# A hybrid recurrent decoder step: the recurrence's rates as their own branch, its scans four a step, the last mLSTM pair one granule later

## The chip, the cores and the metric

The kernel runs on one core of a Trainium2 chip. The metric is the device time of one execution in microseconds (us). The core has a matrix engine (TensorE, PE in the profile; its weight loads are listed as PEld), a vector engine (VectorE, DVE), a scalar engine for activation functions (ScalarE, ACT), a general engine (GpSimd, POOL) and an engine that issues transfers (SyncE, SP). Each takes its own instructions in the order in which the program hands them over, and waits on semaphores that other engines and transfers raise. The 16 DMA engines serve the transfers of all queues.

## The reference

One inference step of a layer of a decoder, for 256 tokens of a prompt and 8 x 4 tokens of samples, 288 columns in all. Three branches share one projection `w_in`, and each is weighed by its own sigmoid gate before `w_out`; an MLP follows.

```python
proj = xn @ P['w_in']                       # D_MODEL = 2048
u, lru_conv_new = causal_conv(lru_x, lru_conv, P['lru_conv_w'], P['lru_conv_b'])
y_lru, lru_h_new = rglru(u, lru_h, ...)
...
h, C_new, n_new, m_new = mlstm_chunked(mq, mk, mv, gates[..., :MLSTM_HEADS], gates[..., MLSTM_HEADS:], ml_C, ml_n, ml_m)
y_ml = jax.nn.sigmoid(m_o) * rmsnorm(h.astype(dt), P['ml_g_norm']).reshape(B, T, MLSTM_WIDTH)
merged = (gate[:, :, 0] * (y_lru @ P['w_br_lru']) + gate[:, :, 1] * (y_gla @ P['w_br_gla'])
          + gate[:, :, 2] * (y_ml @ P['w_br_ml']))
```

The recurrence (RG-LRU) is, per channel,

```python
r = jax.nn.sigmoid((blockdiag(x, w_a) + b_a).astype(f32))
i = jax.nn.sigmoid((blockdiag(x, w_x) + b_x).astype(f32))
log_a = LRU_C * r * jax.nn.log_sigmoid(lam.astype(f32))
a = jnp.exp(log_a)
u = jnp.sqrt(-jnp.expm1(2.0 * log_a)) * (i * x.astype(f32))
# h_t = a_t * h_{t-1} + u_t
```

The factor `log_sigmoid(lam)` depends on weights alone; it is what the kernel calls the rates. The mLSTM branch keeps a matrix memory C of 256 x 256 for each of 4 heads and 8 samples, which is read, used and written back.

## The kernel before

**Layout.** Features lie on the 128 partitions, the 288 columns in the free dimension. A "slot" is an SBUF buffer of 8 x 288 columns. Every large product is done three times in a 32-bit format: a weight tile `raw` of 128 x 1024 is fetched, ACT makes its upper part `hi` (L164) and DVE the rest, `lo = raw - hi` (L171); the activations are split in the same way (`split`, L523 on ACT and L524 on DVE). `stream` (L174 and `stream_`, L183) runs a product in granules: one weight tile, two contraction blocks and four output blocks, so 2 x 4 x 3 = 24 matmuls (L197, L198, L199). There are three buffers each of `raw`, `hi` and `lo`. After the last granule of a block, its four PSUM banks are emptied by the `evac` function that the caller gives; four banks (`pm`) serve the streams, two (`px`) the small products.

**Side work.** `run` (L252) steps a stream granule by granule. After each granule it lets `step` do what a string of letters asks for (`every`: L fetches one tile of the modulation weights `wada` or `wad1`, V multiplies the tiles that have come), and then advances every generator in the list `side` by one `yield`, behind the granule's last matmul and its last `hi` and `lo`. `beside` puts a generator into the list; `finish` runs what is left of it at once.

```python
for g in list(side):
    with tc.high_priority(), ExitStack() as behind:
        for e in ("last", "lo", "hi"):
            behind.enter_context(tc.issue_after(pace[e].ins))
        if next(g, side) is side:
            side.remove(g)
```

The order on SP's queue is the program's own. On the other engines a planner orders the instructions by priority and by its own estimate of times, keeping the `issue_after` constraints. POOL issues the small loads and the stores of states.

**Order of the work.** Six modulation stages apply the condition to x and run six blocks of `w_in` (queries, values, and the recurrence's input `lx`), each over the contraction blocks that the stage adds; stage five (i = 5) adds blocks 12 to 15, two granules for each of its six turns n = 0 to 5. Then come two GATE blocks of 8 granules, the merge of the first branch (`merge`, L1134; for each of 4 blocks one MG block of `w_in` and one block of `wbl`), the MX blocks, the merge of the second branch, two MO blocks (L1566), the merge of the third, `w_out` and the MLP.

**The recurrence,** `lru` (L686), is a side generator from the end of turn n = 4 of stage five. It loads its weights by a POOL transfer, works the rates out of `lam` with small operations on 128 x 8 (L694 to L714), does the convolution (`conv`, L652: first the samples on POOL, then L678 on ACT and L681 on DVE), the two gates for 8 blocks (L729 on TensorE, L723 to L725 on ACT), the roots (L733), the gate products on DVE (L737 to L739), one scan for each of 8 blocks (L749), and the split of the result (L523, L524) as operand of `wbl`. `finish(lru_)` stands between the first MG block, whose gates L1146 moves out of PSUM, and the first `wbl` block.

**The mLSTM,** `mlstm` (L1263), works on its sample states from a table of steps: `do(s, f, ...)` puts a function at step s, and `steps` does one step per granule. States come in 16 tiles, `tiles[n]`, from `mC`; `pair(n)` (L1452) multiplies two tiles with the queries (L1463), updates them (L1479 on TensorE, L1482 and L1484 on DVE) and stores them (L1485). A tile's load waits until the store of the tile four numbers before has been read out. `when(n)` is the step of a pair:

```python
return 5 + n // 2 * 3 + 2 * (n >= 10)
...
do(n + 1 if n < 4 else when(n - 4) + 2, load, n)
```

So pairs 10, 12 and 14 stand at steps 22, 25 and 28, and tiles 14 and 15 are loaded at steps 24. Pair 14 follows the 12th of the 16 MO granules. Behind it, for head 3: `gather` a step after `when(15)`, `squares` and `last` two, the row sums three, their inverse roots four steps after. Then the generator waits for `mos`, set after the MO blocks, and takes four more steps, whose results the first `wbm` block reads; `finish(ml_)` stands ahead of that block, after 8 granules of MG.

Of the kernel before, what the change touches and what calls it, by code (L numbers as in the profile page):

```python
# [53 lines left out]
def trunk(ctx, tc, io):  # L54
    nc = tc.nc
    PSUM = bass.MemoryType.PSUM
    V, S, G, T, Q = nc.vector, nc.scalar, nc.gpsimd, nc.tensor, nc.sync
# [19 lines left out]
    def slot(i, dt=F32):  # L77
        return big.tile([P, 8, N], dt, tag=f"s{i}", name=nm(f"s{i}"))

    def flat(t):  # L80
        return t.rearrange("p a n -> p (a n)")
# [19 lines left out]
    def Pm(n):  # L101
        a, w = POFF[n]
        return par[:, a:a + w]
# [164 lines left out]
    def beside(g):  # L268
        side.append(g)
        return g  # L270

    def finish(g):

        while g in side:
            if next(g, side) is side:
                side.remove(g)
# [406 lines left out]
                yield  # L683


    def lru():  # L686
        wax = slot(3)
        wa = flat(wax)[:, 0:1024].rearrange("p (n d) -> p n d", n=8)
        wx = flat(wax)[:, 1024:2048].rearrange("p (n d) -> p n d", n=8)
        G.dma_start(flat(wax)[:, 0:2048], io["lruw"])  # L690
        uc = slot(4)
        lam = Pm("lam")
        e, s, z, a_ = (sc([P, 8], f"lam{i}", 1) for i in range(4))
        S.activation(e, lam, AF.Abs)  # L694
        S.activation(e, e, AF.Exp, scale=-1.0)
        V.tensor_scalar(s, e, 2.0, None, ALU.add)
        V.reciprocal(s, s)
        yield
        V.tensor_tensor(out=s, in0=s, in1=e, op=ALU.mult)
        V.tensor_tensor(out=z, in0=s, in1=s, op=ALU.mult)  # L700
        V.memset(a_, 1.0 / 19)
        for n in range(8, -1, -1):
            V.tensor_tensor(out=a_, in0=a_, in1=z, op=ALU.mult)
            V.tensor_scalar(a_, a_, 1.0 / (2 * n + 1), None, ALU.add)
        V.tensor_tensor(out=a_, in0=a_, in1=s, op=ALU.mult)
        ls = sc([P, 8], "lam4", 1)
        V.tensor_scalar(ls, lam, 0.0, None, ALU.min)
        V.scalar_tensor_tensor(ls, a_, -2.0, ls, ALU.mult, ALU.add)
        ls2, ls4 = sc([P, 8], "lam5", 1), sc([P, 8], "lam6", 1)
        V.tensor_scalar(ls2, ls, 2.0, None, ALU.mult)  # L710
        V.tensor_scalar(ls4, ls, 4.0, None, ALU.mult)
        hb = sc([P, 2, 8], "hb", 1)
        V.tensor_scalar(hb[:, 0, :], Pm("ba"), 0.5, None, ALU.mult)
        V.tensor_scalar(hb[:, 1, :], Pm("bx"), 0.5, None, ALU.mult)  # L714
        yield from conv(lx, uc, Pm("lcw"), Pm("lcb"), "lst", "o_lconv", slot(1), True)
        thr, thi, tt = slot(5), slot(0), slot(1)
        aa = thr
        ps = {}
        for n in range(8 + 2):
            if n >= 2:  # L720
                i = n - 2
                for j, t in ((0, thr), (1, thi)):
                    S.activation(t[:, i, :], ps.pop((i, j))[:, :N], AF.Tanh, bias=hb[:, j, i:i + 1], scale=0.5)  # L723
                S.activation(tt[:, i, :], thr[:, i, :], AF.Tanh, bias=ls2[:, i:i + 1], scale=ls2[:, i:i + 1])
                exp = S.activation(aa[:, i, :], thr[:, i, :], AF.Exp, bias=ls4[:, i:i + 1], scale=ls4[:, i:i + 1])  # L725
            if n < 8:
                for j, w in ((0, wa), (1, wx)):
                    ps[n, j] = misc()
                    T.matmul(ps[n, j][:, :N], w[:, n, :], uc[:, n, :], start=True, stop=True)  # L729
            yield  # L730
        with tc.issue_after(exp.ins):
            for h in range(4):
                S.activation(tt[:, 2 * h:2 * h + 2], tt[:, 2 * h:2 * h + 2], AF.Sqrt, scale=-0.25)  # L733
        yield
        for h in range(4):
            r = slice(2 * h, 2 * h + 2)
            V.scalar_tensor_tensor(thi[:, r], thi[:, r], 1.0, uc[:, r], ALU.add, ALU.mult)  # L737
            V.tensor_tensor(out=thi[:, r], in0=thi[:, r], in1=tt[:, r], op=ALU.mult)
            V.scalar_tensor_tensor(thi[:, r], aa[:, r], 1.0, thi[:, r], ALU.add, ALU.mult)  # L739
            yield  # L740
        st = sc([P, 8, NB], "lh0", 1)
        V.tensor_tensor(out=st, in0=aa[:, :, NP:N:TS], in1=Pm("h0").rearrange("p (k b) -> p k b", k=8), op=ALU.mult)
        V.tensor_tensor(out=thi[:, :, NP:N:TS], in0=thi[:, :, NP:N:TS], in1=st, op=ALU.add)
        V.memset(aa[:, :, NP:N:TS], 0.0)
        V.memset(aa[:, :, 0:1], 0.0)
        hh = slot(3)
        for h in range(8):
            r = slice(h * N, (h + 1) * N)
            V.tensor_tensor_scan(flat(hh)[:, r], flat(aa)[:, r], flat(thi)[:, r], 0.0, ALU.mult, ALU.add)  # L749
            if h % 2:  # L750
                yield
        ho = sc([P, 8, 9], "lho", 1)
        G.tensor_copy(ho[:, :, 0:1], hh[:, :, NP - 1:NP])
        G.tensor_copy(ho[:, :, 1:9], hh[:, :, NP + 3:N:TS])
        G.dma_start(io["o_lh"], ho)
        ylru.extend([slot(0, F32R), slot(1, F32R)])
        for h in range(4):
            r = slice(2 * h, 2 * h + 2)
            split(ylru[0][:, r], ylru[1][:, r], hh[:, r])
            yield  # L760
# [4 lines left out]
    for i, turn, p in ((2, (5, 4, 0, 1, 2, 3), "F2LL F1FL 2FLL 1 2 ."), (3, (3, 2, 1, 0, 4, 5), "L L . L LV . L L . LLV . ."),  # L765
# [21 lines left out]
        for n, j in enumerate(turn):  # L787
            pace["pins"] = pace["adds"][-5:-4] + [mods] * (n > 0)
            if n == 1:
                pace["hpins"] = [xh1]  # L790
            evac = start_of(5, (0, 2)) if i == 2 and n == 0 else added_to(j)
            run(stream(win, early[j][0], act1, k1, evac, k0=k0, take=None if n else take,
                       keep=kept if n == 5 and i < 5 else None, first=() if n else lead,
                       behind=pace["prod"] if i == 2 and n == 5 else None))
            if i == 5 and n == 4:
                lru_ = beside(lru())
    pace.update(pins=(), hpins=())
    visit()
# [464 lines left out]
    def mlstm():  # L1263
# [34 lines left out]
        for t in range(2):  # L1298
            for q in range(2):
                p = misc()  # L1300
                for i in range(4):
                    n = 4 * q + i
# [5 lines left out]
        p = misc()  # L1308
        for h in range(4):
            for e in range(2):  # L1310
                n = 2 * h + e
# [3 lines left out]
        p = misc()  # L1315
        for h in range(4):
            for e in range(2):
                n = 2 * h + e
# [3 lines left out]
        for t in range(2):  # L1322
            for q in range(2):
                p = misc()
                for i in range(4):
                    n = 4 * q + i
                    T.matmul(p[:, i * P:(i + 1) * P], mc[:, n, t * P:(t + 1) * P], bdk[:, n * P:(n + 1) * P], start=True, stop=True)
                for i in range(2):
                    h = 2 * q + i
# [7 lines left out]
        for n in range(8):  # L1337
            p = misc()
# [6 lines left out]
        p = misc()  # L1345
# [3 lines left out]
        p = misc()  # L1349
# [9 lines left out]
        p = misc()  # L1359
        for h in range(4):  # L1360
            for e in range(2):
                n = 2 * h + e
# [7 lines left out]
        for h in range(4):  # L1370
            p = misc()
# [6 lines left out]
            p = misc()  # L1378
            for e in range(2):
                n = 2 * h + e  # L1380
                T.matmul(p[:, 0:256], mc[:, n, 0:P], tf[:, n, 0:NP], start=e == 0, stop=e == 1)
            for e in range(2):
                n = 2 * h + e
# [6 lines left out]
            for d in range(2):  # L1390
                p = misc()
# [7 lines left out]
            p = misc()  # L1399
# [6 lines left out]
            p = misc()  # L1406
# [101 lines left out]
            at.setdefault(s, []).append(lambda: f(*a))  # L1508

        def when(n):  # L1510
            return 5 + n // 2 * 3 + 2 * (n >= 10)

        do(0, part, kp, ks, 0, K_LO)
        do(0, part, vp, vs[:, 0:256], 0, V_LO)
# [115 lines left out]
    with tc.high_priority():  # L1630
        for k in range(KT):
            f = row(("ar", "mr")[k % 2])
            E = V if k < 2 else G
            h, l, sh = xh2[:, k, :], xl2[:, k, :], mod[:, SH2, k, 0:1]
# [190 lines left out]
```

## Time and profile before

| what | us |
|---|---|
| median of 3 timed runs (lowest to highest) | 1946.62 (1945.56 to 1949.12) |
| the profiled execution, its own time | 1948.79 |
| span of the profiled execution, first to last instruction | 1946.7 |
| DVE busy in the span | 1032.8 |
| ACT busy in the span | 808.2 |

The profile shows one execution. Its span leaves out what lies before the first and after the last instruction, here 1948.79 - 1946.7 = 2.1 us. Matmuls are pipelined, so that a matmul listed with 0.29 us can start 0.13 us after the one before; the rate is read from starts. A row of the timeline gives start, duration, engine, line, operation, tiles out<-in and count, and in brackets the idle time of the engine before it and what ended it. A row of the grouped view gives the busy time of a group, the mean in ns, and the idle time before. A row of the table of stretches gives the stretch from the span's start, its length, the engine's busy time and count, the granted TensorE clock, the share of time in which the DMA engines were busy, and GB/s.

### The profile page before, as it was taken

The page shows a single profiled execution, that of the slowest core. Times are in us where ns is not written, and L with a number is a line of the kernel's source. Part 1 is how long each engine was busy: PE and PEld are TensorE (multiplying, and loading weights), DVE is VectorE, ACT ScalarE, POOL GpSimd, SP SyncE. Part 2 cuts the span into 40 slices and gives each one's busy share as a digit, 9 for nine tenths or more (in the row PEclk, how much of TensorE's full clock was granted, in tenths as well). Part 3 has the DMA queues.
Part 4 walks back from the last instruction along what each step waited for, and adds up shares of the span by engine and source line. Part 5 has one row for each costly group of instructions (what it writes and reads, how often), then busy time and mean ns, then how long its engine had stood idle before and what let it go on. Part 6 is the DMA issues. An engine that isn't in the chain of part 4 may idle for free.

```text
span 1946.7 us, 35923 instructions
## 1 busy us (share of the span) xinstructions
PE 1923.7 (99%) x15068; PEld 1829.7 (94%) x15068; DVE 1032.8 (53%) x1595; ACT 808.2 (42%) x1128; POOL 242.1 (12%) x334
## 2 busy tenths in 40 slices
PE   8999999999999999999999999999999999999997
PEld 6898988999999999899999899999999999999997
DVE  6665747545673466654454554445454444454565
ACT  5333465344554354343333454443333333343433
POOL 0000101011042112001122431000000000000101
PEclk9999999999999999999999999999999999999999
DMA  9997856557443468777788464454444444454452
GB/s 392 380 355 278 310 189 232 200 191 258 162 155 109 163 207 310 259 275 270 273 312 316 162 221 155 161 171 163 162 163 163 163 163 167 169 166 170 161 173 106
DMA packets 110065, 416.42 MB, mean 214 GB/s; under 512 B 11632, under 2 KB 11808, under 8 KB 106192
## 3 DMA queue, kind: packets, MB, share of 16 engines
q1 hardware_dynamic: 100800, 381.55, 55.2%
q0 software_dynamic: 8096, 29.19, 4.2%
q10 hardware_dynamic: 1008, 3.39, 0.5%
q8 instruction: 118, 1.93, 0.4%
q14 instruction: 43, 0.35, 0.1%
HBM read 397.27 MB, written 16.81 MB: 213 GB/s over the span
## 4 chain that ended last, share of the span: by engine, by line
PE 97%; DMA 1%; DVE 1%; ACT 1%; issue 0%; SPq 0%; DVEq 0%; POOL 0%; ACTq 0%; POOLq 0%
PE mm L197 29%; PE mm L199 28%; PE mm L198 28%; PE pa L341 4%; DMA s<-wad 1%; DMA s<-mC 1%; PE px L1479 0%; PE pi L1463 0%; PE px L729 0%; PE px L1008 0%; PE px L1393 0%; PE px L128 0%; PE px L848 0%; PE px L1403 0%; PE mm L234 0%
## 5 line engine op out<-in xcount | busy, mean ns | idle before, releaser
L171 DVE TENSOR_TENSOR lo<-raw,hi 128x1024 fp32r<-128x1024 f32 x448 | 549.1, 1228 | 569.1 <-ACT hi L164 544.2
L164 ACT ACTIVATE hi<-raw 128x1024 fp32r<-128x1024 f32 x444 | 470.3, 1060 | 801.8 <-PE mm L198 649.3
L197 PE MATMUL mm<-xh,hi 128*128 128x288 f32 x2528 | 746.4, 299 | 0.1
L198 PE MATMUL mm<-xl,hi 128*128 128x288 f32 x2528 | 742.8, 296 | 0.0
L199 PE MATMUL mm<-xh,lo 128*128 128x288 f32 x2528 | 732.2, 295 | 0.7 <-DVE lo L171 0.6
L197 PE MATMUL mm<-s,hi 128*128 128x288 f32 x1664 | 491.3, 297 | 1.1 <-ACT s L1146 1.1
L197 PEld LDWEIGHTS mm<-xh,hi 128*128 128x128 f32 x2528 | 472.3, 188 | 19.0 <-issue 12.3
L198 PE MATMUL mm<-s,hi 128*128 128x288 f32 x1664 | 488.5, 295 | 0.0
L199 PE MATMUL mm<-s,lo 128*128 128x288 f32 x1664 | 477.8, 295 | 0.0
L198 PEld LDWEIGHTS mm<-xl,hi 128*128 128x128 f32 x2528 | 474.7, 188 | 1.3
L199 PEld LDWEIGHTS mm<-xh,lo 128*128 128x128 f32 x2528 | 471.7, 188 | 2.3 <-DVE lo L171 1.2
L197 PEld LDWEIGHTS mm<-s,hi 128*128 128x128 f32 x1664 | 312.0, 188 | 6.7 <-issue 5.0
L198 PEld LDWEIGHTS mm<-s,hi 128*128 128x128 f32 x1664 | 312.5, 188 | 0.3
L199 PEld LDWEIGHTS mm<-s,lo 128*128 128x128 f32 x1664 | 308.8, 188 | 0.1
L171 DVE TENSOR_TENSOR lo<-s,hi 128x1024 fp32r<-128x1024 f32 x80 | 98.0, 1225 | 113.4 <-ACT hi L164 113.4
L164 ACT ACTIVATE hi<-s 128x1024 fp32r<-128x1024 f32 x80 | 84.9, 1061 | 142.4 <-PE mm L198 141.7
L1653 POOL TENSOR_TENSOR t<-t 128x288 f32<-128x288 f32 x64 | 60.1, 950 | 639.2 <-ACT t L1652 639.2
L603 DVE TENSOR_TENSOR s<-s,mm 128x288 f32<-128x288 f32 x92 | 39.9, 452 | 51.5 <-PE mm L199 50.4
L1165 POOL TENSOR_TENSOR s<-s,t 128x288 f32<-128x288 f32 x32 | 36.2, 1158 | 186.5 <-DVE t L1164 186.5
L1669 DVE TENSOR_TENSOR s<-s,mm 128x288 f32<-128x288 f32 x96 | 40.3, 450 | 33.9 <-PE mm L199 32.6
L341 PE MATMUL pa<-s,silc 128*32 128x64 f32 (+3 forms) x832 | 50.9, 373 | 0.2 <-DMA s<-wad 0.2
L524 DVE TENSOR_TENSOR s<-t,s 128x288 fp32r<-128x288 f32 x64 | 33.8, 568 | 15.5 <-ACT s L523 15.5
(403 smaller groups left out, 1157.0 us busy)
## 6 DMA issues: line engine op xcount, KB each, us to landing
raw<-win SPq DMA_DIRECT2D x188, 512.0 KB, 4.4
raw<-wf SPq DMA_DIRECT2D x176, 512.0 KB, 4.1
s<-wf SPq DMA_DIRECT2D x80, 512.0 KB, 3.6
s<-wada SPq DMA_DIRECT2D x26, 1024.0 KB, 8.8
s<-wad SPq DMA_DIRECT2D x24, 1024.0 KB, 10.4
ag<-wada SPq DMA_DIRECT2D x22, 1024.0 KB, 6.0
raw<-wout SPq DMA_DIRECT2D x32, 512.0 KB, 5.4
st<-wada SPq DMA_DIRECT2D x20, 512.0 KB, 6.7
```

What stands on the lines that cost most here:

```text
L164: pace["hi"] = S.activation(hi, raw, AF.Copy)
L171: pace["lo"] = V.tensor_tensor(out=lo[:, r], in0=raw[:, r], in1=hi[:, r].bitcast(F32), op=ALU.subtract)
L197: T.matmul(pss[m][:, :N], hi[:, kk, ms], xh, start=k == k0 and not take, stop=False)
L198: T.matmul(pss[m][:, :N], hi[:, kk, ms], xl, start=False, stop=False)
L199: pace["last"] = T.matmul(pss[m][:, :N], lo[:, kk, ms], xh, start=False, stop=k == kt - 1 and keep is None)
L341: pace["prod"] = T.matmul(ps[32 * j:32 * j + 32, h * w // 4:(h + 1) * w // 4], silu_c(k), v[:, j], start=k == 0 and h == 0, stop=k == KT - ...
L524: pace["mod"] = V.tensor_tensor(out=dst_l[:, r], in0=src[:, r], in1=dst_h[:, r].bitcast(F32), op=ALU.subtract)
L603: pace["adds"].append(V.tensor_tensor(out=dst[:, base + m, :], in0=dst[:, base + m, :], in1=p, op=ALU.add))
L1165: G.tensor_tensor(out=a, in0=a, in1=t, op=ALU.add)
L1653: G.tensor_tensor(out=r, in0=r, in1=r, op=ALU.mult)
L1669: V.tensor_tensor(out=a, in0=a, in1=p, op=ALU.add)
```

## The change

Three edits, all to when things are done; the operations and their operands stay the same.

- The rates leave `lru` and become a generator of their own, `lru_rates`, which starts after turn n = 0 of stage five, five turns ahead of `lru`, and is finished ahead of it. In place of the step that it took, `lru` has a `yield` before the convolution.
- In `lru`, the `yield` between the roots and the first gate product goes, and the scans are done four to a step instead of two.
- `when(n)` gives one more for n >= 14, so the last pair goes to step 29, and what hangs on `when(15)` follows by one step. No load depends on it.

```diff
-    def lru():
-        wax = slot(3)
-        wa = flat(wax)[:, 0:1024].rearrange("p (n d) -> p n d", n=8)
-        wx = flat(wax)[:, 1024:2048].rearrange("p (n d) -> p n d", n=8)
-        G.dma_start(flat(wax)[:, 0:2048], io["lruw"])
-        uc = slot(4)
+    rates = []
+
+    def lru_rates():
         lam = Pm("lam")
         e, s, z, a_ = (sc([P, 8], f"lam{i}", 1) for i in range(4))
         S.activation(e, lam, AF.Abs)
...
         V.tensor_scalar(hb[:, 1, :], Pm("bx"), 0.5, None, ALU.mult)
+        rates.extend((ls2, ls4, hb))
+
+    def lru():
+        wax = slot(3)
+        wa = flat(wax)[:, 0:1024].rearrange("p (n d) -> p n d", n=8)
+        wx = flat(wax)[:, 1024:2048].rearrange("p (n d) -> p n d", n=8)
+        G.dma_start(flat(wax)[:, 0:2048], io["lruw"])
+        uc = slot(4)
+        yield
         yield from conv(lx, uc, Pm("lcw"), Pm("lcb"), "lst", "o_lconv", slot(1), True)
+        ls2, ls4, hb = rates
         thr, thi, tt = slot(5), slot(0), slot(1)
...
                 S.activation(tt[:, 2 * h:2 * h + 2], tt[:, 2 * h:2 * h + 2], AF.Sqrt, scale=-0.25)
-        yield
         for h in range(4):
...
             V.tensor_tensor_scan(flat(hh)[:, r], flat(aa)[:, r], flat(thi)[:, r], 0.0, ALU.mult, ALU.add)
-            if h % 2:
+            if h % 4 == 3:
                 yield
...
+            if i == 5 and n == 0:
+                rates_ = beside(lru_rates())
             if i == 5 and n == 4:
+                finish(rates_)
                 lru_ = beside(lru())
...
         def when(n):
-            return 5 + n // 2 * 3 + 2 * (n >= 10)
+            return 5 + n // 2 * 3 + 2 * (n >= 10) + (n >= 14)
```

## The prediction

> **What bounds the kernel now.** The page first: TensorE is busy for almost the whole span, and the chain that ended last runs through it.
>
> ```profile
> span 1946.7 us, 35923 instructions
> ...
> PE 1923.7 (99%) x15068; PEld 1829.7 (94%) x15068; DVE 1032.8 (53%) x1595; ACT 808.2 (42%) x1128; POOL 242.1 (12%) x334
> ...
> PE 97%; DMA 1%; DVE 1%; ACT 1%; issue 0%; SPq 0%; DVEq 0%; POOL 0%; ACTq 0%; POOLq 0%
> ```
>
> So only TensorE's idle time can be won, 1946.7 - 1923.7 = 23 us. Next the list of TensorE's waits (engine, line, releaser: total, times, longest).
>
> ```profile
> PE pi L537 <- DVE t L533: 5.7, 1, 5.7
> PE pi L1463 <- DMA s<-mC: 1.8, 1, 1.8
> PE mm L197 <- ACT s L1146: 1.1, 1, 1.1
> PE mm L199 <- DVE lo L171: 0.6, 1, 0.6
> ```
>
> They hold 9.2 us; nearly all the rest lies before the first matmul and after the last, which the change does not touch. The first and the last of the four fall in the opening, ahead of the edits. Two are left, and each lies where one edit works: the 1.1 us at the end of the first MG block, where the recurrence ends, and the 1.8 us ahead of the last mLSTM pair. Then the table of stretches (busy TensorE, count, granted clock, DMA share, GB/s): one in the last modulation stage, one behind it, three around the pair.
>
> ```profile
> 160.00:180.00 20.00, 20.00 (x153) 1.00 0.73 268
> ...
> 200.00:220.00 20.00, 20.00 (x154) 1.00 0.95 337
> ...
> 796.20:799.62 3.42, 1.64 (x21) 1.00 1.02 418
> 799.62:803.03 3.41, 3.41 (x16) 0.50 1.02 418
> 803.03:806.44 3.41, 3.41 (x28) 1.00 0.12 44
> ```
>
> Stage five and what follows it have no hole. At the pair there is a hole of 3.42 - 1.64 = 1.78 us, and right behind it 3.41 us at half the clock. The matmuls show what that costs.
>
> ```profile
> 796.36 0.29 PE L199 MATMUL mm<-xh,lo 128*128 128x288 f32 x1
> 798.44 1.07 PE L1463 MATMUL pi<-s,s 128*32 128x257 f32 x16 [1.78 <-DMA s<-mC]
> ...
> 800.33 0.44 PE L197 MATMUL mm<-xh,hi 128*128 128x288 f32 x1
> 800.57 0.44 PE L198 MATMUL mm<-xl,hi 128*128 128x288 f32 x1
> ...
> 804.74 0.30 PE L197 MATMUL mm<-xh,hi 128*128 128x288 f32 x1
> 804.87 0.29 PE L198 MATMUL mm<-xl,hi 128*128 128x288 f32 x1
> ...
> 805.24 0.29 PE L199 MATMUL mm<-xh,lo 128*128 128x288 f32 x1
> ```
>
> A matmul starts every 0.24 us at half clock (800.33 to 800.57) and every 0.13 at full (804.74 to 804.87), so one such interval loses 3.41 x (1 - 0.133 / 0.24) = 1.52 us. By this reading the two places hold 1.78 + 1.52 + 1.09 = 4.39 us, 0.23% of the time. Whether they can be collected is the question.
>
> **The last pair.** `when(14)` goes from step 28 to 29. A step comes after one granule, 24 matmuls x 0.133 = 3.2 us. Its loads, from `when(10)` and `when(11)`, do not move; tiles 14 and 15 still land at 798.4. TensorE will instead run granule 13 of the MO blocks from 796.5 to 799.7, at full clock, and then find the tiles there. The pair itself takes 1.6 us at full clock: an earlier one shows it.
>
> ```profile
> 770.37 1.07 PE L1463 MATMUL pi<-s,s 128*32 128x257 f32 x16
> ...
> 771.95 0.30 PE L197 MATMUL mm<-xh,hi 128*128 128x288 f32 x1
> ```
>
> So TensorE wants granule 14 at 799.7 + 1.6 = 801.3. What is late next is that granule's weight tile. SP's issues, the DMA view narrowed to the issue at 787.05, and what ACT and DVE do with the tile:
>
> ```profile
> 785.02 0.38 SPq L380 DMA_DIRECT2D ag<-wada  x1
> ...
> 786.31 0.38 SPq L380 DMA_DIRECT2D s<-wada  x1
> 787.05 0.66 SPq L155 DMA_DIRECT2D raw<-win  x1
> ...
> raw<-win SPq DMA_DIRECT2D x1, 512.0 KB, 15.9
> ...
> 803.00 1.06 ACT L164 ACTIVATE hi<-raw 128x1024 fp32r<-128x1024 f32 x1 [3.04 <-DMA raw<-win]
> ...
> 804.09 1.23 DVE L171 TENSOR_TENSOR lo<-raw,hi 128x1024 fp32r<-128x1024 f32 x1 [2.02 <-ACT hi L164]
> ```
>
> The tile needs 15.9 us, from 787.05 to 802.9, since the DMA engines are full (share 1.02, 418 GB/s) with two 1 MB `wada` tiles, the mC tiles and their stores. ACT starts the moment it lands, DVE right after, and at 805.24 TensorE uses `lo`. These transfers were asked for before the pair or by halvings that don't wait for it, so the edit moves none of them. Already before, granule 14 could go no sooner than 805.24; the pair's wait and the half clock lay inside time that its weights took anyway. After, TensorE idles from 801.3 to 804.06 (`hi` done) and, two matmuls on, until 805.24, 3.6 us instead of 1.78. Won is only what the pair still had to do behind 805.24: one issue pair of L1479, 2 x 0.12 = 0.24 us.
>
> Lost may be a half-clock interval behind the new hole: between 0 and 1.52 us. The nearest rows: 1.78 us of idle brought one, 1.09 us (below) none. 3.6 us is beyond the first, so I expect one. The one here began 1.2 us behind the end of its hole (799.62 against 798.44); one that begins inside a hole costs less, so I take **1.2 us** of the 1.52. [...]
>
> Gather, squares and row sums of head 3 come one granule later. Before, they end at step 32, the last of the MO blocks; after, at step 33, the first of eight MG granules, and the four output steps take 34 to 37, before `finish(ml_)` at 40. Cost nothing. Without that cover it would be up to a granule, 3.2 us. The pair's stores too go a granule later on POOL's queue, where no load stands behind them.
>
> **The recurrence's end.** Before, `lru` has 31 steps and 2 + 16 + 8 = 26 granules until `finish(lru_)`: the last scans and all splits come at the end. After, it has 28: the roots join the first gate step, the four scan steps become two, so scans and splits come three granules sooner and two splits are left. What that end costs now, on ACT, TensorE and DVE:
>
> ```profile
> 304.03 2.41 ACT L523 ACTIVATE s<-s 128x576 fp32r<-128x576 f32 x4 [2.83 <-DVE s L749]
> 306.35 1.04 ACT L164 ACTIVATE hi<-raw 128x1024 fp32r<-128x1024 f32 x1
> 307.29 0.99 ACT L1146 ACTIVATE s<-mm 128x288 f32<-128x288 f32 x3
> ...
> 307.73 0.40 PE L197 MATMUL mm<-s,hi 128*128 128x288 f32 x1 [1.09 <-ACT s L1146]
> ...
> 300.65 3.35 DVE L749 TENSOR_TENSOR_SCAN s<-s,s 128x288 f32<-128x288 f32 x5
> 303.91 1.21 DVE L171 TENSOR_TENSOR lo<-raw,hi 128x1024 fp32r<-128x1024 f32 x1
> 305.03 2.76 DVE L524 TENSOR_TENSOR s<-s,s 128x576 fp32r<-128x576 f32 x4
> ...
> 276.00:308.00 32.00, 28.56 (x45) 1.00 0.65 235
> ```
>
> The splits wait for the scans, keep ACT for 2.41 us, one halving follows, and only then L1146 empties the four PSUM banks; TensorE resumes as the first is free. DVE sets the pace: 28.56 of 32 us. It has 3.44 us of idle, nearly all in waits for `hi` ahead of the gate products; work that comes earlier in its queue fills those. I take the end 3 us sooner, splits done by about 304 to 305 on DVE and 303 to 304 on ACT, and the wait of **1.09 us gone**. Bounds: 0 to 1.09 won, or lost as in the slower rival.
>
> **The rates.** Thirty small DVE operations and two of ACT move from the first two recurrence steps to the second block of stage five.
>
> ```profile
> L704 DVE TENSOR_SCALAR lam<-lam 128x8 f32<-128x8 f32 x9 | 1.5, 165 | 0.0
> L703 DVE TENSOR_TENSOR lam<-lam,lam 128x8 f32<-128x8 f32 x9 | 1.5, 162 | 0.0
> ...
> L695 ACT ACT_TABLE_LOAD x1 | 1.3, 1283 | 0.0
> ...
> 158.00:196.00 38.00, 21.36 (x42) 1.00 0.77 282
> ```
>
> Eighteen take 3.0 us, so thirty some 5 to 6; DVE has 38 - 21.36 = 16.6 us idle there, which hides them. If a halving or PSUM addition stood behind the first of them while ACT loads its table, 1.3 us could show. Where they leave, around 200 to 228, TensorE had no hole, so nothing is won. I take 0. The new first yield of `lru` leaves its convolution at the step that it had.
>
> **Sum** on the profiled execution, whose own time was 1948.79 (span 1946.7 and 2.1 around it): -1.09 - 0.24 + 1.2 = **-0.13**, 1948.66. That execution stands 2.17 above the median of the timed runs, 1946.62; on the median the change gives **1946.5 us**. A measurement of this kernel can tell about 0.2%, 3.9 us, from no change.
>
> **The rivals.**
> *The weights come in time, full gain.* Both holes and the half clock go: -4.39, 1942.2. For it: timed runs may have less DMA pressure than the profiled one. Against: the 15.9 us landing, independent of the pair. 17%.
> *Handed to the weights without half clock:* -1.33, 1945.3. For it: the wait of 1.09 us brought no half clock, and the second part of the new hole is no longer; against: 1.78 us was enough once. 20%. [...]
> *The edit of the recurrence does not do what it says:* ACT still splits just ahead of L1146; the 1.09 stays: -0.24 + 1.2, 1947.6. For it: two splits still follow the block. 10%.
> *Slower: scans ahead of a halving.* Four scans in one step occupy DVE for 4 x 0.738 = 2.95 us (DVE's grouped rows give 5.4 us for eight), in front of a `lo` that, in the row at 303.91, ends at 305.1, 1.5 us before the matmuls up to 306.6 are through. Put ahead of `lo` there, or where the reserve is smaller, TensorE waits 1.5 to 2.95 us, and then another half clock comes. At most 2.95 + 1.52 - 1.09 - 0.24 + 1.2 = +4.34, 1951.0. It decides as soon as the reserve of `lo` is under about 0.4 us. 13%.
> *The forecast:* 40%.
>
> ```profile
> L749 DVE TENSOR_TENSOR_SCAN s<-s,s 128x288 f32<-128x288 f32 x8 | 5.4, 738 | 0.0
> ```
>
> **Chances.** Only the full gain passes 3.9 us downward (1942.2 against 1942.7): faster 17%. Forecast, no half clock and unchanged recurrence lie within: 70%. Slower 13%. The forecast's half clock of 0 to 1.52 alone spans 1945.3 to 1946.8; the range must take in the full gain, while the slow rival may stay out: **1942.0 to 1949.5**.
>
> **What the profile after would show.** Step one right: no wait of L1463 on mC, but one of L197 or L199 on `hi` or `lo` of some 3 us just behind the pair, the tile landing about 16 us after its issue, then a stretch at 0.5 clock. Wrong: that tile lands before 801, or TensorE runs through. Step two right: L523 ends before 305, no wait on L1146; wrong: a wait on `lo` L171 between 285 and 310. Step three right: no new hole from 160 to 190. The forecast falls if other streams are reordered and open holes elsewhere.

## The result, and the profile after

Fifteen runs of each kernel: the changed kernel takes **1944.02 us** in the median (1943.18 to 1945.29), the one before 1946.86 (1945.48 to 1951.34). The ratio is 0.9985 with an interval of 0.9978 to 0.9992: 2.84 us, 0.15%, inside what the prediction called no change, and 2.5 us below its number. From profiled execution to profiled execution it is more: 1948.79 to 1944.02, 4.77 us. That the two differences disagree turns out to be the main finding.

The page of the changed kernel has the same shape as before: TensorE all but full, and the end hanging on it.

```profile
span 1942.2 us, 35921 instructions
...
PE 1921.3 (99%) x15068; PEld 1828.6 (94%) x15068; DVE 1033.7 (53%) x1595; ACT 808.2 (42%) x1128; POOL 243.4 (13%) x334
...
PE 96%; DMA 2%; DVE 1%; ACT 1%; issue 0%; SPq 0%; DVEq 0%; ACTq 0%
```

Its list of TensorE's waits (engine, line, releaser: total, times, longest). Lines behind L755 are 9 higher than before: L1463 is now L1472, L1479 L1488, L1482 L1491, L1146 L1155.

```profile
PE pi L537 <- ACT t L535: 5.6, 1, 5.6
PE px L1488 <- DVE s L1491: 0.8, 1, 0.8
PE mm L199 <- DVE lo L171: 0.6, 1, 0.6
```

Both waits that the prediction worked on are gone: the 1.1 us on ACT at the recurrence's end, and the 1.8 us on mC at the pair. A smaller one has come, 0.8 us of L1488 on L1491. The table of stretches shows the half clock gone too (length, busy TensorE, count, granted clock, DMA share, GB/s):

```profile
796.20:799.62 3.42, 3.42 (x36) 1.00 1.14 368
799.62:803.03 3.41, 3.41 (x29) 1.00 0.88 349
803.03:806.44 3.41, 2.66 (x20) 1.00 0.51 162
276.00:308.00 32.00, 31.87 (x238) 1.00 0.58 221
158.00:196.00 38.00, 38.00 (x320) 1.00 0.76 274
```

**Where the time went.** Every profile of this study has the same 12,576 large matmuls (L197 to L199), so the start of the k-th can be compared between kernels. I cut the execution at four of them, numbers 1536, 1920, 4224 and 4800 (counted from 0), which in the kernel before start at 293.58, 352.94, 763.88 and 863.00 us. The second stretch holds the recurrence's end, the fourth the last pairs and the mLSTM's closing steps.

| profile | to the first | to 1536 | **1536 to 1920** | to 4224 | **4224 to 4800** | to the last | outside the span |
|---|---|---|---|---|---|---|---|
| before | 36.26 | 257.32 | 59.36 | 410.94 | 99.13 | 1068.84 | 2.1 |
| changed | 36.23 | 257.32 | 58.34 | 410.94 | 95.73 | 1068.85 | 1.8 |

The two stretches that the edits touch lost 1.02 and 3.40 us, 0.3 us went outside the span, and nothing else moved: 4.7 of the 4.77. The 3.40 us are the hole of 1.78 and the half clock of 1.52, less the new hole of 0.75, and about 0.85 more, which two groups of small products give (below).

The recurrence's end in the timeline of the changed kernel:

```profile
296.40 3.31 DVE L755 TENSOR_TENSOR_SCAN s<-s,s 128x288 f32<-128x288 f32 x5
...
299.76 2.05 DVE L755 TENSOR_TENSOR_SCAN s<-s,s 128x288 f32<-128x288 f32 x3
...
301.84 2.41 ACT L523 ACTIVATE s<-s 128x576 fp32r<-128x576 f32 x4 [3.85 <-DVE s L755]
...
302.98 2.76 DVE L524 TENSOR_TENSOR s<-s,s 128x576 fp32r<-128x576 f32 x4
...
306.05 0.98 ACT L1155 ACTIVATE s<-mm 128x288 f32<-128x288 f32 x3
```

The splits start at 301.84 on ACT instead of 304.03 and at 302.98 on DVE instead of 305.03. ACT is free for the emptying of the PSUM banks at 306.05, and the first `wbl` matmul comes at 306.49 instead of 307.73, with no wait.

The pair in the same timeline:

```profile
798.75 1.07 PE L1472 MATMUL pi<-s,s 128*32 128x257 f32 x16
799.75 0.50 PE L1488 MATMUL px<-s,s 128*128 128x256 f32 x2
800.09 0.40 PE L1488 MATMUL px<-s 128*128 128x256 f32 x2
...
801.54 1.06 ACT L164 ACTIVATE hi<-raw 128x1024 fp32r<-128x1024 f32 x1 [7.60 <-DMA raw<-win]
...
802.63 1.23 DVE L171 TENSOR_TENSOR lo<-raw,hi 128x1024 fp32r<-128x1024 f32 x1 [7.43 <-ACT hi L164]
...
803.78 0.87 DVE L1491 SCALAR_TENSOR_TENSOR s<-s,csb,px 128x256 f32<-128x256 f32 x2
...
804.70 0.51 PE L1488 MATMUL px<-s,s 128*128 128x256 f32 x2 [0.75 <-DVE s L1491]
```

The late weight tile is there as foretold: issued at 785.74, landed at 801.44, 15.7 us. But the large matmuls of the granule behind the pair run without a gap from 800.33 until the next granule starts at 803.52, and that tile has its `lo` only at 802.63 + 1.23 = 803.86. It is the weight of the granule **after** that one. What it delays is something else: the pair's first update (L1491) stands in DVE's queue behind the `lo` that waits for the tile, and the third of the pair's four groups of update matmuls (L1488) waits for the PSUM bank that this update empties. The hole is 0.75 us, and no half clock follows it: the granted clock is 1.00 from 803.03 to 820.00.

### The profile page after: what moved, and what is told of

It reads as the page before. It is cut to its first block, busy times and chain, and to the rows that moved or that the text cites. A ratio compares the mean times of both kernels' runs of the same rounds, so it can differ in the third digit from the quotient of the medians.

```text
span 1942.2 us, 35921 instructions
## 1 busy us (share of the span) xinstructions
PE 1921.3 (99%) x15068; PEld 1828.6 (94%) x15068; DVE 1033.7 (53%) x1595; ACT 808.2 (42%) x1128; POOL 243.4 (13%) x334
## 4 chain that ended last, share of the span: by engine, by line
PE 96%; DMA 2%; DVE 1%; ACT 1%; issue 0%; SPq 0%; DVEq 0%; ACTq 0%
PE mm L197 29%; PE mm L199 28%; PE mm L198 28%; PE pa L341 4%; DMA raw<-win 1%; DMA s<-wad 1%; PE px L736 0%; PE px L1488 0%; PE px L1017 0%; PE pi L1472 0%; DMA s<-x 0%; PE px L1402 0%; PE px L128 0%; PE px L857 0%; PE px L1412 0%; PE pi L473 0%
## 5 line engine op out<-in xcount | busy, mean ns | idle before, releaser
L197 PE MATMUL mm<-xh,hi 128*128 128x288 f32 x2528 | 746.7, 299 | 0.1
L199 PE MATMUL mm<-xh,lo 128*128 128x288 f32 x2528 | 732.8, 296 | 0.7 <-DVE lo L171 0.6
L197 PE MATMUL mm<-s,hi 128*128 128x288 f32 x1664 | 491.8, 298 | 0.0
L197 PEld LDWEIGHTS mm<-xh,hi 128*128 128x128 f32 x2528 | 472.4, 188 | 18.1 <-issue 12.2
L199 PE MATMUL mm<-s,lo 128*128 128x288 f32 x1664 | 478.8, 295 | 0.0
L199 PEld LDWEIGHTS mm<-xh,lo 128*128 128x128 f32 x2528 | 471.7, 188 | 1.8 <-DVE lo L171 1.2
L197 PEld LDWEIGHTS mm<-s,hi 128*128 128x128 f32 x1664 | 312.4, 188 | 5.5 <-issue 5.0
L199 PEld LDWEIGHTS mm<-s,lo 128*128 128x128 f32 x1664 | 309.2, 188 | 0.3
L1174 POOL TENSOR_TENSOR s<-s,t 128x288 f32<-128x288 f32 x32 | 36.2, 1158 | 179.9 <-DVE t L1173 179.9
L341 PE MATMUL pa<-s,silc 128*32 128x64 f32 (+3 forms) x832 | 50.9, 373 | 0.4 <-DMA s<-wad 0.3
```

The lines of the kernel that those rows point to most:

```text
L197: T.matmul(pss[m][:, :N], hi[:, kk, ms], xh, start=k == k0 and not take, stop=False)
L199: pace["last"] = T.matmul(pss[m][:, :N], lo[:, kk, ms], xh, start=False, stop=k == kt - 1 and keep is None)
L341: pace["prod"] = T.matmul(ps[32 * j:32 * j + 32, h * w // 4:(h + 1) * w // 4], silu_c(k), v[:, j], start=k == 0 and h == 0, stop=k == KT - ...
L1174: G.tensor_tensor(out=a, in0=a, in1=t, op=ALU.add)
```

## The experiments

After the result two theories stood against each other. **One:** the wait on mC with its half clock belongs to the order of the kernel before, so that most of its runs have it, and the pair's edit brings most of the gain. **The other:** the profiled execution of before was an unlucky one (it lies 2.17 us above the median), usual runs have no such wait, and the gain of the medians comes from the recurrence. In the expectations of the first four runs below, P is the first theory, and R or Q the second. Times below are medians with their spread and count; "before" is the kernel before on the same chip.

### The pair alone

The kernel before with the last edit only.

```diff
-            return 5 + n // 2 * 3 + 2 * (n >= 10)
+            return 5 + n // 2 * 3 + 2 * (n >= 10) + (n >= 14)
```

> The kernel before with the pair's edit alone (when(n) + 1 for n >= 14). Theory P (the pair's wait for its tile and the half clock behind it are what the change removed): the 1.78 us wait of L1463 and the 0.5 clock stretch are gone, the 1.09 us wait on L1146 stays, about -3.4 us in the profiled span (1946.7 to about 1943.3), median 1.5 to 2.5 us under that of before, and a narrow spread of the runs (under 2.5 us between lowest and highest). Rival R (the profiled run of before was an exception, and the median moved by the recurrence's edits): median within 1 us of before, spread as wide as that of before (4 us and more). Rival W (the wait is handed to the late weight tile, as predicted): a hole of about 3 us just behind the pair, span within 0.5 us of before.

Measured: 1945.82 (1944.57 to 1947.69, 11 runs) against 1946.09 (1945.08 to 1949.52, 33), ratio 0.9996 (0.9987 to 1.0005): 0.27 us less, not to be told from nothing. The list of waits:

```profile
PE mm L197 <- ACT s L1146: 1.3, 1, 1.3
...
PE px L1479 <- DVE s L1482: 0.4, 1, 0.4
```

The recurrence's wait is untouched, the update's is there, and of the 1.5 to 2.5 us of the first theory there is no trace in the median. The spread of 3.1 us fits neither forecast.

### The recurrence without the pair

The changed kernel with the pair back at step 28.

```diff
-            return 5 + n // 2 * 3 + 2 * (n >= 10) + (n >= 14)
+            return 5 + n // 2 * 3 + 2 * (n >= 10)
```

> The changed kernel with the pair put back to step 28: the recurrence's edits alone. Theory P: no wait on the MG block's evacuation at the end of the recurrence, -1.1 to -1.25 us there, the pair's wait and half clock still seen in most runs, median 1.0 to 1.3 us under before, spread wide (4 us and more). Rival R: median 2 us or more under before and a narrow spread.

Measured: 1944.26 (1943.82 to 1946.03, 11 runs) against the same 1946.09, ratio 0.9990 (0.9982 to 0.9999): 1.83 us less. Neither wait is in its list, the one on mC included, though the pair stands where it stood. The 1.83 lies between what the two theories gave (1.0 to 1.3, and 2 or more). With the pair's 0.27 this makes 2.10.

### The changed kernel once more

The same text as the changed kernel, beside the experiments on the closing steps.

> The changed kernel once more, beside the three below. Theory Q (formed on the first four runs): the recurrence's edits give 1.5 to 1.9 us in every run, the pair's edit only takes away a wait that comes in those runs in which tile 15 lands late. Then this is 1.8 to 2.4 us under before in the median, and its highest run stands under 1946. Rival P (the pair's edit is worth its 3.3 us in every run): 3 us and more under before.

Measured: 1943.81 (1943.02 to 1944.69, 11 runs) against 1945.92 (1945.16 to 1948.29, 33), ratio 0.9989 (0.9980 to 0.9998): 2.11 us less, close to the sum of the two parts, though each part has an interval of 3.3 to 3.5 us. The wait of L1488 is 1.0 us here.

### The kernel before, looked at once more

> The kernel before, profiled once more. Theory P (the wait of L1463 on mC belongs to the order: tile 15 lands behind the moment at which the pair wants it in most runs): a wait of 1 to 2.5 us on mC, a half-clock interval behind it or none, span 1945 to 1947. Theory Q (the first profiled run was an unlucky one): no wait of L1463 on mC, tile 15 landing before the pair's first matmul, no half-clock interval in mid-run, span 1943.6 to 1944.4; the wait of L197 on ACT L1146 of 0.8 to 1.3 us stays.

Measured: one run of 1946.3, in the middle of the 21 others on that chip (median 1946.28), span 1944.2. Its list of waits:

```profile
PE pi L537 <- DVE t L533: 6.1, 1, 6.1
PE mm L197 <- ACT s L1146: 1.3, 1, 1.3
PE mm L199 <- DVE lo L171: 0.6, 1, 0.6
```

No wait on mC, no half clock, and the pair follows without a gap, as two rows of the timeline and two of the table of stretches show:

```profile
797.28 0.29 PE L199 MATMUL mm<-xh,lo 128*128 128x288 f32 x1
797.50 1.07 PE L1463 MATMUL pi<-s,s 128*32 128x257 f32 x16
...
796.00:799.41 3.41, 3.41 (x35) 1.00 1.01 408
799.41:802.82 3.41, 3.41 (x28) 1.00 1.01 411
```

The landing of mC's tile 15 against the end of the large matmuls ahead of the pair, read from the transfers and matmuls of four profiles:

| profile | tile 15 issued | landed | pair could start | margin |
|---|---|---|---|---|
| before, first profile | 787.84 | 798.39 | 796.66 | -1.7 |
| before, second | 786.52 | 794.78 | 797.50 | +2.7 |
| recurrence only | 784.97 | 793.45 | 795.36 | +1.9 |
| changed (a granule later) | 786.18 | 796.46 | 798.75 | +2.3 |

In all seven other profiles of kernels with the pair at step 28, tile 15 lands 1.6 to 2.7 us ahead of the pair. The stretch from 4224 to 4800 takes 99.13 us in the first profile of the kernel before, **95.75** in the second, 95.75 with the recurrence alone, 95.73 in the changed kernel. The 3.40 us between the two first profiles are the luck of one execution, and the edit wins next to nothing in a usual one.

It may win the unlucky ones. In all three profiles with the pair at step 29, tile 15 landed behind the end of the 12th MO granule, where a pair at step 28 would have asked for it: by 0.84 us in the changed kernel, by 0.04 in its second profile and by 0.13 with the pair alone. There the later step covered it. Of the kernel before, 5 of the 87 runs in these studies and 3 of the 15 beside the result lie over 1.9 us above their median; of the changed kernel, in 26 runs, none lies more than 1.3 above. Only one such long run was profiled, so that the late tile is the cause of the others is argued, not shown. Against it stand the pair alone, whose slowest run lies 1.9 above its median, the kernel with the pair later still (2.3), and three runs, each of a kernel with the pair at step 28, that lie 4.5 to 5.1 above, more than the 3.40 us of the profiled one.

### Scans and roots without the rates

The kernel before with the second edit only.

```diff
-        yield
         for h in range(4):
             r = slice(2 * h, 2 * h + 2)
...
-            if h % 2:
+            if h % 4 == 3:
                 yield
```

> The kernel before with the scans four a step and the roots in the step of the first gate product, rates where they were. Theory: this is the whole of the recurrence's gain, the 1.09 us wait goes, splits end 2 us sooner, median -1.0 to -1.3 us. Rival (the rates carry it): wait stays, median within 0.4 us.

Measured: 1944.94 (1944.36 to 1946.72, 11 runs) against 1946.09, ratio 0.9995 (0.9987 to 1.0004): 1.15 us less, as expected, though the interval holds no change as well. The trace is clearer: the wait at the recurrence's end is gone, and ACT splits from 300.37.

### Four scans a step alone

```diff
-            if h % 2:
+            if h % 4 == 3:
```

> The kernel before with four scans a step instead of two, nothing else (two steps fewer in the recurrence; the roots keep their yield). If the scans alone let the splits off ACT in time: no wait on L1146, -0.9 to -1.2 us against before, span 1942.7 to 1943.2. If the roots' step is needed too: part of the wait stays (0.3 to 0.8 us) and the time is -0.3 to -0.8 us. The time outside the span stays at about 2.1 us, since the rates are not moved.

Measured: 1945.94 (1945.21 to 1949.75, 10 runs) against 1946.28 (1945.13 to 1949.15, 21), ratio 0.9999 (0.9990 to 1.0008). The wait stays, at 1.0 us, outside both forecasts. DVE's timeline says why:

```profile
298.23 2.06 DVE L749 TENSOR_TENSOR_SCAN s<-s,s 128x288 f32<-128x288 f32 x3
300.20 1.20 DVE L171 TENSOR_TENSOR lo<-raw,hi 128x1024 fp32r<-128x1024 f32 x1
301.32 3.35 DVE L749 TENSOR_TENSOR_SCAN s<-s,s 128x288 f32<-128x288 f32 x5
```

Three scans, one halving, five scans: the order is that of the kernel before, whose groups stood at 297.56 and 300.65, and this execution runs 0.7 to 0.9 us behind it from the opening on. With two yields fewer DVE keeps the same order. With the roots' yield gone as well (the experiment above) the order is another:

```profile
294.94 3.31 DVE L748 TENSOR_TENSOR_SCAN s<-s,s 128x288 f32<-128x288 f32 x5
...
298.30 2.04 DVE L748 TENSOR_TENSOR_SCAN s<-s,s 128x288 f32<-128x288 f32 x3
...
300.38 1.22 DVE L171 TENSOR_TENSOR lo<-raw,hi 128x1024 fp32r<-128x1024 f32 x1
```

All eight scans stand ahead of the halving. So the scans' edit alone does nothing, and the end opens only with the roots' step. Whether that step would do without the scans' edit, or both are needed, was not tried.

### The rates alone

The changed kernel with the pair, the scans and the roots as before; only `lru_rates` stays a branch of its own, and the first yield of `lru`.

```diff
+        yield
         for h in range(4):
...
-            if h % 4 == 3:
+            if h % 2:
                 yield
...
-            return 5 + n // 2 * 3 + 2 * (n >= 10) + (n >= 14)
+            return 5 + n // 2 * 3 + 2 * (n >= 10)
```

> The kernel before with the rates alone as a branch of their own from stage five (scans two a step, roots with their own step). Theory: nothing, median within 0.4 us of before, the 1.09 us wait at the end of the first MG block stays. Rival: freeing DVE of the thirty operations around 200 to 228 lets the recurrence end sooner, and the wait goes here already (-1.1).

Measured: 1945.15 (1944.78 to 1946.58, 11 runs) against 1946.09, ratio 0.9996 (0.9987 to 1.0004): 0.94 us less, more than expected. A third of it is not in the span at all: the run's time less its span is 1.78 us in the median of its runs, and 2.11 in 87 runs of the kernel before. The same holds for every kernel of the study: with the rates moved, medians of 1.76 to 1.80 and no run above 1.84; without, 2.10 to 2.13 and none under 2.05. What lies in those 0.33 us no profile shows, since they are before the first or behind the last instruction. The rest of the 0.94 is within what the opening varies by itself (36.2 to 37.1 us to the first large matmul) and 0.3 us of the recurrence's wait, which is 0.8 here; it is 0.8 as well in two kernels whose recurrence is that of before (closing steps later, pair one earlier).

### Where the closing products stand

In the profile of the changed kernel the row sums of head 3 (L890) and the products of the modulation weights (L341) alternate; in the first profile of before (L881, L341) they stood apart. TensorE's timeline, before:

```profile
812.35 0.69 PE L881 MATMUL px<-s,ones 128*32 128x288 f32 x6
...
813.42 1.16 PE L881 MATMUL px<-s,ones 128*32 128x288 f32 x10
...
817.63 1.07 PE L341 MATMUL pa<-ag,silc 128*32 128x512 f32 x8
818.51 1.04 PE L341 MATMUL pa<-s,silc 128*32 128x512 f32 x8
```

And changed:

```profile
812.18 1.09 PE L341 MATMUL pa<-ag,silc 128*32 128x512 f32 x8
813.06 0.69 PE L890 MATMUL px<-s,ones 128*32 128x288 f32 x8
813.55 1.08 PE L341 MATMUL pa<-s,silc 128*32 128x512 f32 x8
814.40 0.70 PE L890 MATMUL px<-s,ones 128*32 128x288 f32 x8
```

Before, the large matmuls around them start at 812.12 and 812.96, 813.20 and 814.51, 817.40 and 819.48; after, at 811.96 and 815.04. Less the 0.13 us of the large matmul ahead, the same 32 products cost 0.71 + 1.18 + 1.95 = 3.84 us before and 2.95 us after, 0.9 less. That is about the 0.85 left over above. The same reckoning gives 3.81 to 3.84 us in all seven profiles in which they stand apart, the second look among them, and 2.95 in all five in which they alternate. In the changed kernel this gain is used up: the two L1488 matmuls behind the hole cost 1.25 us between the large ones (1.50 in its second profile) against 0.24 in the second look, so the stretch is as long as before. To see whether it can be had without the pair, the kernel before with only head 3's closing steps a granule later:

```diff
-            e = when(4 * h + 3)
+            e = when(4 * h + 3) + (h == 3)
```

> The kernel before with the pair at step 28 and only head 3's gather, squares, sums and roots one step later. Theory Q: the row sums L881 then alternate with the tiles that step V multiplies instead of standing alone between streams, worth 0.6 to 0.9 us there as in the changed kernel; the pair's wait stays possible. Median 0.5 to 0.9 us under before. Rival: the order of these small products costs nothing, within 0.3 us.

Measured: 1945.05 (1944.29 to 1950.12, 11 runs) against 1945.92, ratio 0.9997 (0.9988 to 1.0006): 0.87 us less. The products alternate again and cost 2.95 us. But the stretch 4224 to 4800, 95.45 us, is only 0.30 shorter than in the second look: the four products of the gather a little ahead (L896), which also wait for updates on DVE, cost 1.01 us here and 0.36 there. The rest of the 0.87 lies in parts of the run that this edit does not touch, and the interval holds no change as well. So the 0.9 us of the products is shown by the traces; that the median falls by it is not.

### The pair two later

```diff
-            return 5 + n // 2 * 3 + 2 * (n >= 10) + (n >= 14)
+            return 5 + n // 2 * 3 + 2 * (n >= 10) + 2 * (n >= 14)
```

> The changed kernel with the pair at step 30 instead of 29. Theory Q: tile 15 has three more us of reserve that nobody needs, and the hole of 0.75 us (L1488 waits for the update L1491, which stands behind a lo that waits for a late weight tile) goes; the closing sums leave the place beside step V. Median within 0.5 us of the changed kernel. Rival P: reserve still matters, 1 us and more faster.

Measured: 1945.36 (1945.08 to 1947.68, 11 runs) against 1945.92, ratio 0.9999 (0.9990 to 1.0008), 1.55 us slower than the changed kernel beside it, where at most 0.5 was expected: a miss. The update's wait is gone as expected, but the closing steps went along: the modulation products of two tiles now mix one by one, with the four products of the gather (L905) between them, around 811 to 813, and the row sums stand alone.

```profile
817.52 0.69 PE L890 MATMUL px<-s,ones 128*32 128x288 f32 x6
...
818.60 1.16 PE L890 MATMUL px<-s,ones 128*32 128x288 f32 x10
```

The stretch takes 96.85 us against 95.99 for the changed kernel beside it.

### The pair one earlier

```diff
-            return 5 + n // 2 * 3 + 2 * (n >= 10)
+            return 5 + n // 2 * 3 + 2 * (n >= 10) - (n >= 14)
```

> The kernel before with the last pair one granule earlier, at step 27. If it is the landing of tile 15 that the pair waits for, TensorE asks 3.3 us sooner for data that comes no sooner: a wait of 1.3 to 5 us in every run, half clock behind most of them, median 2 to 6 us over before. If the wait has another cause (the order of updates, PSUM), within 1 us of before.

Measured: 1946.80 (1945.88 to 1948.24, 10 runs) against 1945.92, ratio 1.0004 (0.9995 to 1.0013). It was meant to bring the wait on mC into every run. But the planner put the pair only 7 large matmuls earlier, at 795.92, tile 15 had landed at 794.41, and no wait on mC came; a wait of 0.9 us of L896 on the update came instead, and the products stood apart. The time stayed within 1 us of before, but that does not speak for another cause of the wait: the run says nothing on the landing, and so the price of a late tile rests on the one profile that has it.

### What is left: both gains without the queue behind `lo`

The recurrence's three edits, the pair at its old step, and only head 3's closing steps a granule later.

```diff
-            return 5 + n // 2 * 3 + 2 * (n >= 10) + (n >= 14)
+            return 5 + n // 2 * 3 + 2 * (n >= 10)
...
-            e = when(4 * h + 3)
+            e = when(4 * h + 3) + (h == 3)
```

> The recurrence's three edits with the last pair where it was before (step 28), and only head 3's closing steps one granule later. If what the pair's edit wins in a usual run is the row sums that alternate with the products of V, this keeps that gain and does without the pair's hole behind lo (0.75 to 1.0 us): 1943.2 to 1943.7, that is 0.3 to 0.7 us faster than the changed kernel and 2.4 to 3.0 faster than before, if tile 15 lands in time. If tile 15 lands late in part of the runs, the median stays in that range and the slowest run passes 1945.5. If e5's -0.87 was chance and not the sums, it comes out with the recurrence alone: 1944.0 to 1944.3.

Measured: **1943.41** (1942.88 to 1948.21, 11 runs) against 1946.28 (1945.13 to 1949.15, 21), ratio 0.9989 (0.9980 to 0.9997): 2.87 us less, the changed kernel on another chip 2.11 less. The stretch 4224 to 4800 takes 94.69 us, the shortest of all. In its timeline the updates stand ahead of the late `lo`:

```profile
797.54 0.87 DVE L1491 SCALAR_TENSOR_TENSOR s<-s,csb,px 128x256 f32<-128x256 f32 x2 [0.84 <-PE px L1488]
...
798.48 0.87 DVE L1491 SCALAR_TENSOR_TENSOR s<-s,csb,px 128x256 f32<-128x256 f32 x2
...
800.81 1.06 ACT L164 ACTIVATE hi<-raw 128x1024 fp32r<-128x1024 f32 x1 [3.30 <-DMA raw<-win]
...
801.04 0.40 PE L1488 MATMUL px<-s,s 128*128 128x256 f32 x2
...
801.90 1.23 DVE L171 TENSOR_TENSOR lo<-raw,hi 128x1024 fp32r<-128x1024 f32 x1 [2.42 <-ACT hi L164]
```

So L1488 finds its bank empty at 801.04, while the weight tile, landed at 800.73, is still being halved. The price is in the spread: 3 of 11 runs lie over 1.6 us above the median, one 4.8 above; of the kernel before on that chip it is 2 of 21, the highest 2.9 above. The 0.76 us that it has over the changed kernel is smaller than either interval (0.9980 to 0.9997 is 3.3 us), and the two were not run on one chip.

The stretches of all experiments (us), as in the table above:

| profile | to the first | 1536 to 1920 | 4224 to 4800 | median outside the span |
|---|---|---|---|---|
| before, second look | 36.98 | 59.61 | 95.75 | 2.11 (87 runs) |
| four scans a step alone | 37.11 | 59.24 | 96.11 | 2.12 |
| scans and roots | 36.33 | 58.03 | 96.01 | 2.13 |
| rates alone | 36.38 | 59.03 | 95.87 | 1.78 |
| recurrence (three edits) | 36.36 | 58.03 | 95.75 | 1.76 |
| pair alone | 36.72 | 59.70 | 95.47 | 2.10 |
| changed, again | 36.41 | 58.03 | 95.99 | 1.80 |
| closing steps later | 36.55 | 59.03 | 95.45 | 2.12 |
| pair two later | 36.43 | 58.20 | 96.85 | 1.78 |
| pair one earlier | 36.53 | 59.12 | 96.87 | 2.13 |
| recurrence and closing steps | 36.34 | 58.68 | 94.69 | 1.79 |

## Why the prediction was right in range and wrong in steps

**The recurrence's end, -1.09: right in size, wrong in its reason.** Six profiles with the roots' yield or the scans as before take 59.03 to 59.70 us there, besides the first (59.36); the six with both edits 58.03 to 58.68. From the middle of one group to that of the other it is 1.1 us, as expected (1.09). The splits came 2.1 to 2.2 us sooner instead of 3. The step "the four scan steps become two, so scans and splits come three granules sooner" did not hold: four scans a step alone moved nothing, because DVE's order stayed. With the roots' yield gone as well, the last gate product (L739 before) is done ahead of the last halving before the scans and no longer behind it, and all scans come ahead of the next. The slower rival, scans ahead of a halving, happened in its first half: all eight stand ahead of a `lo`, and TensorE did not wait, since that `lo` was done with time to spare.

**The rates, 0: right in the span, 0.33 missed outside.** DVE's table of stretches in the changed kernel has for the second block of stage five

```profile
158.00:196.00 38.00, 25.14 (x72) 1.00 0.76 274
```

so 30 operations more and 3.8 us, and TensorE's table above is full there (38.00 of 38.00): the cover held. What no row of before could have told is the 0.33 us outside the span.

**The last pair, -0.24 + 1.2: wrong.** The step that failed is "What is late next is that granule's weight tile". There are three weight buffers, and the tile that lands 15.9 us after its issue is not the next granule's but the one after; I matched a late landing with the next matmul that used a `lo`, and did not count the tiles between. The rows shown say so already: that halving ends at 804.09 + 1.23 = 805.32, behind the matmul at 805.24 that was to use it. In the kernel before its granule, the 15th of MO, starts only at 808.40. So the granule behind the pair waited for nothing, the hole was 0.75 instead of 3.6 us, and the half clock, priced at 1.2, did not come. In that execution the wait and the half clock were real cost, and they went: -3.40 instead of +0.96. By the profiled execution the rival "the weights come in time, full gain" (-4.39) came nearest, with 4.77; it had been given 17%.

**The sum, carried over to the median: wrong too, the other way.** "That execution stands 2.17 above the median" was kept as a constant offset. It was the wait of the pair and its half clock, of which the second look, in the middle of the runs, has none: taking its 95.75 for the stretch, the first profile had 3.4 us that the median did not pay, of which a shorter opening gave back 0.7. So the full gain could not show in the median, and two errors partly cancelled: a gain that was there in the profile and not foreseen, and an offset that went with it. That the time fell into the range is luck as far as the pair goes, since the range reached so low only for the full gain. -0.13 was predicted, and -2.84 and -2.11 were measured, of which the recurrence's end gives about 1.1, the time outside the span 0.33, and the pair 0 to 0.3. The remaining 0.4 to 1.4 us stays open; part of it is the kernel before, whose median beside the result (1946.86) lies 0.6 to 0.9 above those beside the experiments (1945.92 to 1946.28).

**The clock.** The hole of 1.78 us in the first profile was followed by 3.41 us at half clock (0.50 from 799.62 to 803.03); the holes of 0.4 to 1.3 us behind the opening of these profiles were followed by none (granted clock 1.00). With one case on that side, what brings the half clock stays open: whether it is the length of the hole, and from which length on, no run shows.

## What to carry to other kernels

Before pricing a wait that ends on a transfer, look at how far the profiled execution lies from the median: an execution that is slow by about the size of the wait may be one of few that have it, and then its removal need not move the median. To say which work a late tile holds up, count the buffers between its landing and its use, and look as well at what stands behind the waiting instruction in the queue of the engine that prepares it. A yield in a side branch moves only what the planner then really orders differently; the order of the operations on the limiting engine shows it, the number of steps does not.

## What the runs showed of the hardware

- One hole of 1.78 us was followed by an interval of 3.41 us at half clock (0.50); holes of up to 1.3 us behind the opening were followed by none, in any of the thirteen profiles (1.00).
- The weight tile of 512 KB that lands behind the last pair takes 15.9 us from issue to landing in the first profile of the kernel before, with the transfers at 418 GB/s from 796.20 to 803.03, and 15.7 us in that of the changed kernel; mC's tile 15 takes 8.3 to 10.6 us in the four profiles of the table of landings. With the pair at step 28, that tile's margin varies from -1.7 to +2.7 us, enough to decide whether TensorE waits.
- The same 32 small products cost TensorE 0.9 us less where the two groups alternate than where each stands alone between large matmuls (2.95 us in five profiles, 3.81 to 3.84 in seven). TensorE returns to the large ones three times there and once here; that the returns are what costs is argued from this count, not shown.
- With thirty-two small operations moved some 40 us earlier, ahead of a branch, the time outside the span is 0.33 us less: at most 1.84 us in every run of the five kernels that do so, at least 2.05 in every run of the others whose span is on record. Its cause is not known.
